# A two-layer attention encoder on one core: block A's value products in two passes of 128 stationary columns, the merging chain a slot later, the first chunk's gate six slots later

## The chip, the cores and the metric

The kernel runs on one core of a Trainium2 chip. PE is the matrix engine (TensorE), DVE the vector engine, ACT the scalar engine, POOL is GpSimd, SP issues the DMAs. The metric is the time of one execution on the device in microseconds (us); of several runs the median counts. 1463.04 us is the median of three runs of the kernel before.

## What is computed

Two encoder layers over x of 1024 positions by 1024 features, all in float32. Each layer normalises x, projects it into the inputs of three attention blocks, A (4 heads), B (6) and C (6), lets each attend, multiplies each block's output by a silu gate and adds the output projection to x. Block A, which the change touches, merges three dilated windows by their log-sum-exp:

```python
DILATED_PATTERNS = ((128, 1), (512, 4), (2048, 16))
for window, dil in DILATED_PATTERNS:
    ...
    m = jnp.max(s, axis=-1, keepdims=True)
    p = jnp.exp(s - m)
    den = jnp.sum(p, axis=-1, keepdims=True)
    o = jnp.einsum('bndhij,bnjdhe->bnidhe', (p / den).astype(v.dtype), vw)
    lse = (m + jnp.log(den))[..., 0]
    ...
w = jax.nn.softmax(jnp.stack(lses, axis=0), axis=0)
out = jnp.sum(w[..., None] * jnp.stack(outs, axis=0), axis=0)
...
y = jnp.concatenate([ya, yb, yc], axis=-1)      # each times its silu gate
x = x + y @ w_out[l]
```

## The kernel before

A float32 operand of a matmul is held as two rounded parts, a high and a low one, and a product is made of three passes: high by high, high by low, low by high. For the values of a head the stationary tile `w` has 128 columns, the 64 high ones in `w[:, LO]` and the 64 low ones in `w[:, HI]`.

Block A treats a head as 8 classes of positions (the four-step pattern, "class" below) and as windows of neighbouring positions. Per head `a_s` makes scores on PE (L897 to L903), DVE adds a table and takes the maximum (L910, L913), `a_exp` is on ACT. The two normalisations are merged by the chain `a_x1` to `a_x5`: DVE L929, PE L937 (a permutation), DVE L944 to L951, ACT L956, DVE L962 to L969 (which gives the window scale `sc` and `z`), PE L977 (the permutation back, from `z`), DVE L983 and L986 (the class scale `s2c`). POOL multiplies the weights by the scales, eight window norms L992 from `sc` and eight class norms L996 from `s2c` for a head. Then PE transposes them, L1009 for classes (`a_t`, i 0 to 3) and L1014 to L1020 for windows (i 4 to 7), each block is split by an ACT copy (L782, L1024) and a DVE subtraction (L783, L1026), and `a_v` multiplies by the values: for classes L1038 to L1040, for windows L1051 to L1053, each line one pass with 64 stationary columns into the 64 low partitions of a PSUM accumulator `acc`:

```python
T.matmul(o, w[:, LO], ph[:, s], start=(kb == 0), stop=False)
T.matmul(o, w[:, LO], pl[:, s], start=False, stop=False)
T.matmul(o, w[:, HI], ph[:, s], start=False, stop=(kb == 1))
```

`a_end` brings an accumulator to SBUF: a class half is copied by ACT (L1085) into the 64 partitions of `y` that belong to the head, a window half is added to it by DVE (L1088, through a strided view). Two heads fill one chunk `fc` of `y`; `fin_gate` multiplies it by its gate on POOL (L820 for block A's chunks 0 and 1, strided; L822 else), `fin_split` splits it (ACT L836, POOL L837). Blocks B and C have `soft` (DVE L762 takes the row maximum of PE's L760 products, ACT L769 the exponential), `norm` (DVE L775, POOL L776), transposes L789 and products L801, L802, and end with two ACT copies (L848, L853) and a POOL add (L854). Early parts of the output projection, `f_load` (a weight piece by DMA, split on POOL by L1103 and L1104) and `f_mm` (PE L1116 to L1118), are put between them.

The order is set by a table: `put(slot, f, pri)` puts a call into a numbered slot, and calls are issued slot by slot, in a slot by priority. A scheduler then settles the order on PE, DVE, POOL and SP; ACT keeps the order written. Block A's head h has its class and window transposes in slots `base_a + AT0 + 8*h + i`, its value products `AV` = 2 slots later, its chain at `CHAIN` (slot offset, priority) behind its last scores, and its norms at fixed slots around the transposes. `FA` are the offsets of a chunk's gate and split.

## Time and profile before

| | |
|---|---|
| median of three runs | 1463.04 us (1462.65 to 1463.38) |
| the profiled execution's own time | 1461.05 us |
| its span in the trace | 1459.1 us |
| PE busy | 1443.1 us (99%), 7912 instructions |
| DVE busy | 1094.5 us (75%), 1997 |
| ACT busy | 899.4 us (62%), 1678 |
| POOL busy | 574.3 us (39%), 516 |

Busy shares are means over the whole span. An engine that is 39% busy can still be the one that others wait for in a stretch. The profiled execution is one run, 2.0 us under the median, and the span is 1.95 us less than its time.

### The profile page before, as it was taken

The page shows a single profiled execution, that of the slowest core. Times are in us where ns is not written, and L with a number is a line of the kernel's source. Part 1 is how long each engine was busy: PE and PEld are TensorE (multiplying, and loading weights), DVE is VectorE, ACT ScalarE, POOL GpSimd, SP SyncE. Part 2 cuts the span into 40 slices and gives each one's busy share as a digit, 9 for nine tenths or more (in the row PEclk, how much of TensorE's full clock was granted, in tenths as well). Part 3 has the DMA queues.
Part 4 walks back from the last instruction along what each step waited for, and adds up shares of the span by engine and source line. Part 5 has one row for each costly group of instructions (what it writes and reads, how often), then busy time and mean ns, then how long its engine had stood idle before and what let it go on. Part 6 is the DMA issues. An engine that isn't in the chain of part 4 may idle for free.

```text
span 1459.1 us, 23134 instructions
## 1 busy us (share of the span) xinstructions
PE 1443.1 (99%) x7912; PEld 1227.4 (84%) x7912; DVE 1094.5 (75%) x1997; ACT 899.4 (62%) x1678; POOL 574.3 (39%) x516
## 2 busy tenths in 40 slices
PE   9999999999999999999999999999999999999999
PEld 7998888888888888888889988888888888888887
DVE  7759767488888789994736597574888787899942
ACT  6473234488888769993425723343888886799820
POOL 6204431135455565550322054211454554754500
PEclk9999999999999999999999999999999999999999
DMA  6261136610287821102622611465103688121143
GB/s 223 80 245 59 52 107 207 207 44 30 51 202 204 243 84 51 44 26 75 212 81 90 238 40 47 166 198 156 59 30 76 172 242 235 31 59 30 44 148 121
DMA packets 118134, 171.81 MB, mean 118 GB/s; under 512 B 11520, under 2 KB 73088, under 8 KB 118016
## 3 DMA queue, kind: packets, MB, share of 16 engines
q1 hardware_dynamic: 118016, 170.32, 38.2%
q8 instruction: 63, 1.03, 0.3%
q14 instruction: 55, 0.45, 0.1%
HBM read 109.47 MB, written 60.82 MB: 117 GB/s over the span
## 4 chain that ended last, share of the span: by engine, by line
PE 90%; DVE 4%; ACT 3%; DMA 1%; issue 1%; SPq 0%; POOL 0%; ACTq 0%; DVEq 0%
PE S L760 15%; PE T L789 11%; PE acc L802 6%; PE acc L801 6%; PE T L669 4%; PE T L667 4%; PE T L668 4%; PE S L1262 3%; PE S L1260 3%; PE S L1261 3%; PE S L221 2%; PE S L222 2%; PE S L223 2%; PE T L705 1%; PE T L221 1%
## 5 line engine op out<-in xcount | busy, mean ns | idle before, releaser
L783 DVE TENSOR_TENSOR wl<-T,wh 128x512 fp32r<-128x512 f32 x440 | 297.0, 685 | 69.2 <-ACT wh L782 67.2
L782 ACT ACTIVATE wh<-T 128x512 fp32r<-128x512 f32 x440 | 261.2, 596 | 115.7 <-PE T L789 77.4
L776 POOL TENSOR_SCALAR u<-u,rec 128x1024 f32<-128x1024 f32 x192 | 216.5, 1128 | 277.4 <-DVE rec L775 176.7
L760 PE MATMUL S<-u,u 96*128 96x512 f32 (+1 forms) x960 | 268.7, 409 | 0.5 <-ACT u L769 0.3
L762 DVE TENSOR_REDUCE nmax<-S 128x1 f32<-128x1024 f32 x192 | 233.7, 1217 | 23.7 <-PE S L760 23.2
L789 PEld LDWEIGHTS T<-ident,u 128*128 128x128 f32 x1536 | 190.8, 140 | 49.0 <-DVE wl L783 0.4
L789 PE MATMUL T<-ident,u 128*128 128x128 f32 x1536 | 230.0, 272 | 0.0
L769 ACT ACTIVATE u<-S,nmax 128x1024 f32<-128x1024 f32 x192 | 213.2, 1111 | 0.3
L150 POOL TENSOR_TENSOR wl<-wr,wh 128x512 fp32r<-128x512 f32 (+2 forms) x48 | 75.1, 1567 | 320.4 <-ACT wh L146 314.9
L760 PEld LDWEIGHTS S<-u,u 96*128 96x128 f32 (+1 forms) x960 | 166.7, 189 | 27.9 <-ACT u L769 1.4
L146 ACT ACTIVATE wh<-wr 128x512 fp32r<-128x512 f32 (+2 forms) x96 | 56.9, 596 | 157.6 <-PE S L222 97.3
L667 PE MATMUL T<-u,wh 128*128 128x512 f32 x256 | 102.1, 399 | 0.0
L669 PE MATMUL T<-u,wl 128*128 128x512 f32 x256 | 100.1, 391 | 0.0
L668 PE MATMUL T<-u,wh 128*128 128x512 f32 x256 | 99.9, 390 | 0.0
L801 PE MATMUL acc<-wh,u 128*128 128x512 f32 x192 | 84.5, 440 | 0.0
L801 PE MATMUL acc<-wh,qb 128*128 128x512 f32 x192 | 82.8, 431 | 0.0
L802 PE MATMUL acc<-wl,u 128*128 128x512 f32 x192 | 76.1, 396 | 2.5 <-DVE wl L783 2.5
L802 PE MATMUL acc<-wl,qb 128*128 128x512 f32 x192 | 76.1, 397 | 0.1
L150 DVE TENSOR_TENSOR wl<-wr,wh 128x512 fp32r<-128x512 f32 (+2 forms) x48 | 41.5, 865 | 44.2 <-ACT wh L146 44.2
L1260 PE MATMUL S<-u,qb 128*128 128x512 f32 x186 | 74.1, 398 | 0.0
L1262 PE MATMUL S<-u,qb 128*128 128x512 f32 x186 | 73.2, 394 | 0.0
L1261 PE MATMUL S<-u,qb 128*128 128x512 f32 x186 | 72.9, 392 | 0.0
(294 smaller groups left out, 3342.0 us busy)
## 6 DMA issues: line engine op xcount, KB each, us to landing
u<-qk_c SPq DMA_DIRECT2D x40, 256.0 KB, 4.1
wr<-in_w_g_dram SPq DMA_DIRECT2D x32, 256.0 KB, 2.6
gates<-h SPq DMA_DIRECT2D x32, 256.0 KB, 2.3
qk_c<-u SPq DMA_DIRECT2D x16, 512.0 KB, 4.0
u<-gates SPq DMA_DIRECT2D x16, 512.0 KB, 3.6
qb<-qk_a SPq DMA_DIRECT2D x32, 256.0 KB, 5.9
vb<-u SPq DMA_DIRECT2D x16, 384.0 KB, 3.3
u<-vb SPq DMA_DIRECT2D x12, 512.0 KB, 4.8
```

The costliest lines, as they stand in the source:

```text
L667: T.matmul(ps[half], wh[:, w], xh[k][:, s], start=(k == 0), stop=False)
L668: T.matmul(ps[half], wh[:, w], xl[k][:, s], start=False, stop=False)
L669: T.matmul(ps[half], wl[:, w], xh[k][:, s], start=False, stop=(k == 7))
L760: T.matmul(ps[:, w], q[:, s], k[:, w], start=(i == 0), stop=(i == len(terms) - 1))
L762: V.tensor_reduce(nmax, ps, op=ALU.max, axis=AX.X, negate=True)
L769: A.activation(p, ps, AF.Exp, bias=nmax, accum_out=den)
L776: G.tensor_scalar(p, p, rec, 1.0, ALU.mult, ALU.mult)
L782: A.activation(ph, ps, AF.Copy)
L783: V.tensor_tensor(pl, ps, f32(ph), ALU.subtract)
L789: T.transpose(ps[:, i * P:(i + 1) * P], Pt[hd, 4 * half + i][0][:, j * P:(j + 1) * P], ident)
L801: T.matmul(acc, w, ph, start=(j == 0), stop=False)
L802: T.matmul(acc, w, pl, start=False, stop=(j == 7))
```

## The change

`a_v` takes the whole of `w` as the stationary tile, so that high and low values are multiplied in one pass, the products of the high values arriving in the accumulator's partitions `LO` and those of the low values in `HI`: two passes instead of three. `a_end` has then to add the two halves of the accumulator. For a class half ACT copies both out and POOL adds them (L1087). For a window half ACT copies `HI` out (strided), DVE adds `LO` to it (L1093) and POOL adds the result to `y` (L1094). The temporary is an `H` tile, of which there are now seven. In `CHAIN` the steps `a_x1p` to `a_x5` go one slot later, `a_x1` stays. For chunk 0 (`h == 1`) `fin_gate` and `fin_split` go six slots later. `f_load` goes three slots later (`FL` 5 instead of 8).

```diff
     def H(dt=F32, shape=(P, 512)):
-        return sp.tile(list(shape), dt, tag="H", name=nm("h"), bufs=6)
+        return sp.tile(list(shape), dt, tag="H", name=nm("h"), bufs=7)
...
-                o = accs["a", h, "c"][LO, (i % 2) * 256:(i % 2) * 256 + 256]
+                o = accs["a", h, "c"][:, (i % 2) * 256:(i % 2) * 256 + 256]
...
-                    T.matmul(o, w[:, LO], ph[:, s], start=(kb == 0), stop=False)
-                    T.matmul(o, w[:, LO], pl[:, s], start=False, stop=False)
-                    T.matmul(o, w[:, HI], ph[:, s], start=False, stop=(kb == 1))
+                    T.matmul(o, w, ph[:, s], start=(kb == 0), stop=False)
+                    T.matmul(o, w, pl[:, s], start=False, stop=(kb == 1))
...
-                T.matmul(o, w[rows, LO], ph[rows, cols], start=start, stop=False, skip_group_check=True)
-                T.matmul(o, w[rows, LO], pl[rows, cols], start=False, stop=False, skip_group_check=True)
-                T.matmul(o, w[rows, HI], ph[rows, cols], start=False, stop=stop, skip_group_check=True)
+                T.matmul(o, w[rows], ph[rows, cols], start=start, stop=False, skip_group_check=True)
+                T.matmul(o, w[rows], pl[rows, cols], start=False, stop=stop, skip_group_check=True)
...
             y = pairs[fc][0]
+            t1 = H()
             if what == "c":
-                A.activation(y[rows, half * 512:half * 512 + 512], acc[LO], AF.Copy)
+                out = y[rows, half * 512:half * 512 + 512]
+                A.activation(t1[rows], acc[HI], AF.Copy)
+                A.activation(out, acc[LO], AF.Copy)
+                G.tensor_tensor(out, out, t1[rows], ALU.add)
             else:
                 yv = y.rearrange("p (r s i) -> p s r i", r=4, s=2)[rows, half]
-                V.tensor_tensor(yv, acc[LO].rearrange("p (i r) -> p r i", r=4), yv, ALU.add)
+                tv = t1[rows].rearrange("p (r i) -> p r i", r=4)
+                lo, hi = (acc[part].rearrange("p (i r) -> p r i", r=4) for part in (LO, HI))
+                A.activation(tv, hi, AF.Copy)
+                V.tensor_tensor(tv, lo, tv, ALU.add)
+                G.tensor_tensor(yv, yv, tv, ALU.add)
...
-        FA = (10, 14)
...
-        CHAIN = ((2, 6), (4, 4.5), (5, 0), (5, 1.5), (6, 0), (8, 4.5), (9, 0))
+        CHAIN = ((2, 6), (5, 4.5), (6, 0), (6, 1.5), (7, 0), (9, 4.5), (10, 0))
...
+                FA = (16, 20) if h == 1 else (10, 14)
...
-        F0, FN, FP, FL = -10, 5, 6.5, 8
+        F0, FN, FP, FL = -10, 5, 6.5, 5
```

POOL, layer 0, from the last class norms of head 1 (L996 from `s2c_5197` before, `s2c_5221` after) to the first of head 2; L992 are head 2's window norms. Before:

```order
L996 TENSOR_SCALAR u_4901<-u_4901,s2c_5197 128x256 x2
L992 TENSOR_SCALAR u_4938<-u_4938,sc_5400 128x192
L992 TENSOR_SCALAR u_4938<-u_4938,sc_5400 128x256
L992 TENSOR_SCALAR u_4999<-u_4999,sc_5400 128x256 x2
L992 TENSOR_SCALAR u_5073<-u_5073,sc_5400 128x256 x2
L992 TENSOR_SCALAR u_5151<-u_5151,sc_5400 128x256
L992 TENSOR_SCALAR u_5151<-u_5151,sc_5400 128x192
L996 TENSOR_SCALAR u_4938<-u_4938,s2c_5502 128x256 x2
```

The same place after; L1094 are the window adds of head 0, L1087 the first class add of head 1:

```order
L996 TENSOR_SCALAR u_4893<-u_4893,s2c_5221 128x256 x2
L1094 TENSOR_TENSOR u_5130<-u_5130,h_5352 64x4x128
L1094 TENSOR_TENSOR u_5130<-u_5130,h_5356 64x4x128
L992 TENSOR_SCALAR u_4934<-u_4934,sc_5416 128x192
L992 TENSOR_SCALAR u_4934<-u_4934,sc_5416 128x256
L992 TENSOR_SCALAR u_4991<-u_4991,sc_5416 128x256 x2
L992 TENSOR_SCALAR u_5056<-u_5056,sc_5416 128x256 x2
L992 TENSOR_SCALAR u_5150<-u_5150,sc_5416 128x256
L992 TENSOR_SCALAR u_5150<-u_5150,sc_5416 128x192
L1087 TENSOR_TENSOR u_5130<-u_5130,h_5433 64x512
L996 TENSOR_SCALAR u_4934<-u_4934,s2c_5523 128x256 x2
```

Nothing stood between the norms of the two heads before; now two adds stand ahead of head 2's window norms and one ahead of its class norms.

POOL, layer 0, from the last class norms of head 2 (L996) to the class norms of head 3; L992 are head 3's window norms, L820 the gates of chunk 0. Before:

```order
L996 TENSOR_SCALAR u_5151<-u_5151,s2c_5502 128x256 x2
L820 TENSOR_TENSOR u_5132<-u_5134,u_5132 128x512 x2
L992 TENSOR_SCALAR u_5221<-u_5221,sc_5645 128x192
L992 TENSOR_SCALAR u_5221<-u_5221,sc_5645 128x256
L992 TENSOR_SCALAR u_5293<-u_5293,sc_5645 128x256 x2
L992 TENSOR_SCALAR u_5382<-u_5382,sc_5645 128x256 x2
L992 TENSOR_SCALAR u_5459<-u_5459,sc_5645 128x256
L992 TENSOR_SCALAR u_5459<-u_5459,sc_5645 128x192
L996 TENSOR_SCALAR u_5221<-u_5221,s2c_5719 128x256 x2
L996 TENSOR_SCALAR u_5293<-u_5293,s2c_5719 128x256 x2
```

The same place after; L1087 and L1094 are the new adds, into `u_5130` for heads 0 and 1 and into `u_5669` for head 2:

```order
L996 TENSOR_SCALAR u_5150<-u_5150,s2c_5523 128x256 x2
L1087 TENSOR_TENSOR u_5130<-u_5130,h_5505 64x512
L1094 TENSOR_TENSOR u_5130<-u_5130,h_5609 64x4x128
L820 TENSOR_TENSOR u_5128<-u_5130,u_5128 128x512
L1094 TENSOR_TENSOR u_5130<-u_5130,h_5613 64x4x128
L820 TENSOR_TENSOR u_5128<-u_5130,u_5128 128x512
L1087 TENSOR_TENSOR u_5669<-u_5669,h_5670 64x512
L992 TENSOR_SCALAR u_5207<-u_5207,sc_5650 128x192
L992 TENSOR_SCALAR u_5207<-u_5207,sc_5650 128x256
L992 TENSOR_SCALAR u_5286<-u_5286,sc_5650 128x256 x2
L992 TENSOR_SCALAR u_5367<-u_5367,sc_5650 128x256 x2
L992 TENSOR_SCALAR u_5452<-u_5452,sc_5650 128x256
```

Where the two gates stood alone ahead of head 3's window norms, they now stand among four adds there, and a fifth, head 2's second class add, comes one row further down, ahead of the last window norm.

DVE, layer 0, from the window sums of head 3's chain (L950) to its scale `sc` (L966) and `z` (L969); L1088 are the last adds of head 1. Before:

```order
L950 TENSOR_TENSOR mm_5613<-st_5219 128x8
L951 TENSOR_TENSOR e_5614<-mm_5613,st_5219 128x16
L783 TENSOR_TENSOR wl_5623<-T_5617,wh_5622 128x512
L1088 TENSOR_TENSOR u_5134<-acc_5543,u_5134 64x4x128
L1088 TENSOR_TENSOR u_5134<-acc_5569,u_5134 64x4x128
L962 TENSOR_TENSOR t_5640<-st_5219,e_5614 128x16
L963 TENSOR_TENSOR rc_5641<-t_5640 128x8
L783 TENSOR_TENSOR wl_5655<-T_5649,wh_5654 128x512
L964 RECIPROCAL rc_5641<-rc_5641 128x8
L966 TENSOR_TENSOR sc_5645<-e_5614,rc_5641 128x16
L969 TENSOR_TENSOR z_5647<-sc_5645,order_2206 128x32
```

The same place after; L1093 are the adds out of PSUM that took the place of L1088, of which the first (it stands one row higher) is left out, L944 and L947 begin head 3's chain step, L762 is a row maximum of block C:

```order
L1093 TENSOR_TENSOR h_5613<-acc_5559,h_5613 64x512
L944 TENSOR_TENSOR z_5619<-T_5601,order_2206 128x32 x2
L783 TENSOR_TENSOR wl_5633<-T_5627,wh_5632 128x512
L947 TENSOR_REDUCE st_5205<-z_5619 128x2x8
L950 TENSOR_TENSOR mm_5623<-st_5205 128x8
L951 TENSOR_TENSOR e_5624<-mm_5623,st_5205 128x16
L962 TENSOR_TENSOR t_5645<-st_5205,e_5624 128x16
L963 TENSOR_TENSOR rc_5646<-t_5645 128x8
L762 TENSOR_REDUCE nmax_5690<-S_5685 128x1
L964 RECIPROCAL rc_5646<-rc_5646 128x8
L783 TENSOR_TENSOR wl_5660<-T_5654,wh_5659 128x512
L966 TENSOR_TENSOR sc_5650<-e_5624,rc_5646 128x16
```

The adds out of PSUM now stand ahead of the chain's step, the four tiny operations L950, L951, L962 and L963 follow each other directly, and a row maximum has come between L963 and L964.

## Rows read from the trace of the kernel before

**Rows 1.** The page's chain of work that ended last, by engine:

```profile
PE 90%; DVE 4%; ACT 3%; DMA 1%; issue 1%; SPq 0%; POOL 0%; ACTq 0%; DVEq 0%
```

**Rows 2.** Stretches: from:to and length in us, then each engine's busy us (instructions), PE clock:

```profile
470.22:489.52 19.30, 19.27 (x138) 17.16 (x136) 16.44 (x62) 13.42 (x47) 15.28 (x26) 1.00 0.96 294
489.52:508.61 19.09, 18.49 (x136) 16.44 (x134) 13.52 (x45) 12.93 (x42) 7.25 (x16) 1.00 0.75 209
508.61:523.25 14.64, 12.41 (x102) 10.96 (x100) 12.82 (x26) 7.40 (x16) 8.58 (x15) 1.00 0.69 196
523.25:536.70 13.45, 13.45 (x105) 12.01 (x104) 11.34 (x19) 10.90 (x21) 8.68 (x10) 1.00 0.01 2
...
1212.82:1231.89 19.07, 18.47 (x135) 16.43 (x134) 13.52 (x45) 12.91 (x42) 7.25 (x16) 1.00 0.71 197
```

**Rows 3.** Timeline of PE: start, us, what; in brackets idle time before and its releaser:

```profile
490.75 0.41 PE L937 MATMUL T<-z,order 128*128 128x64 f32 x2 [0.60 <-DVE wl L1026]
...
509.73 0.41 PE L937 MATMUL T<-z,order 128*128 128x64 f32 x2 [0.50 <-DVE wl L1026]
...
517.95 0.38 PE L977 MATMUL T<-z,order 128*128 128x32 f32 x2 [1.73 <-DVE z L969]
```

**Rows 4.** Timeline of POOL and DVE, 470 to 518 us:

```profile
513.50 3.07 POOL L820 TENSOR_TENSOR u<-u,u 128x512 f32<-128x512 f32 x2 [5.45 <-issue]
...
513.99 1.11 DVE L962 TENSOR_TENSOR t<-st,e 128x16 f32<-128x16 f32 x1
515.13 1.46 DVE L963 TENSOR_TENSOR rc<-t 128x8 f32<-128x8 f32 x1
...
517.40 0.18 DVE L966 TENSOR_TENSOR sc<-e,rc 128x16 f32<-128x16 f32 x1
...
472.01 1.30 POOL L854 TENSOR_TENSOR u<-h,h 64x512 f32<-64x512 f32 x1
...
472.43 0.90 DVE L950 TENSOR_TENSOR mm<-st 128x8 f32<-128x8 f32 x1
```

**Rows 5.** Timeline of PE, passes of 256 columns, and one change of column count:

```profile
475.00 0.28 PE L1040 MATMUL acc<-wh,qb 128*64 128x256 f32 x1
475.12 0.28 PE L1038 MATMUL acc<-wh,qb 128*64 128x256 f32 x1
...
469.38 0.28 PE L898 MATMUL S<-qb,u 128*128 128x256 f32 x1
469.50 0.28 PE L902 MATMUL S<-qb,u 128*128 128x256 f32 x1
...
480.96 0.28 PE L898 MATMUL S<-qb,u 128*128 128x192 f32 x1
481.24 0.30 PE L1038 MATMUL acc<-wh,qb 128*64 128x256 f32 x1
```

**Rows 6.** Groups by line: line, engine, operation, form, count | busy us, mean ns of one:

```profile
L1085 ACT ACTIVATE u<-acc 64x512 f32<-64x512 f32 x16 | 9.4, 590 | 0.6
...
L1088 DVE TENSOR_TENSOR u<-acc,u 64x512 f32<-64x512 f32 x16 | 10.2, 676 | 0.1
...
L762 DVE TENSOR_REDUCE nmax<-S 128x1 f32<-128x1024 f32 x192 | 233.7, 1217 | 23.7 <-PE S L760 23.2
...
L776 POOL TENSOR_SCALAR u<-u,rec 128x1024 f32<-128x1024 f32 x192 | 216.5, 1128 | 277.4 <-DVE rec L775 176.7 <-PE T L789 47.6 <-PE acc L802 21.7
...
L854 POOL TENSOR_TENSOR u<-h,h 64x512 f32<-64x512 f32 x24 | 30.9, 1287 | 14.2 <-ACT h L853 14.1
```

**Rows 7.** Timeline of POOL, norms of head 3:

```profile
517.74 3.57 POOL L992 TENSOR_SCALAR u<-u,sc 128x192 f32<-128x192 f32 x8 [1.17 <-issue]
521.28 3.68 POOL L996 TENSOR_SCALAR u<-u,s2c 128x256 f32<-128x256 f32 x8
```

**Rows 8.** Timeline of PE, head 1's last value matmul, and block C's second half:

```profile
512.21 0.22 PE L1053 MATMUL acc<-wh,qb 64*64 64x128 f32 x1
...
548.75 0.60 PE L789 MATMUL T<-ident,u 128*128 128x128 f32 x4
```

More of the change, by code (lines that the diff above doesn't have):

```diff
@@ L1049, in mm @@
             def mm(half, q0, w, rows, cols, start=False, stop=False):
-                o = accs["a", h, half][LO, q0 * P:q0 * P + (cols.stop - cols.start)]
-                T.matmul(o, w[rows, LO], ph[rows, cols], start=start, stop=False, skip_group_check=True)
-                T.matmul(o, w[rows, LO], pl[rows, cols], start=False, stop=False, skip_group_check=True)
-                T.matmul(o, w[rows, HI], ph[rows, cols], start=False, stop=stop, skip_group_check=True)
+                o = accs["a", h, half][:, q0 * P:q0 * P + (cols.stop - cols.start)]
+                T.matmul(o, w[rows], ph[rows, cols], start=start, stop=False, skip_group_check=True)
+                T.matmul(o, w[rows], pl[rows, cols], start=False, stop=stop, skip_group_check=True)
             full = slice(0, P)
```

## Prediction

> **What bounds the kernel now.** I read the chain of waits first: nine tenths of the chain that ended last lie on PE [rows 1]. So a shorter PE program shortens the kernel wherever nothing else sets the time, and the question is where PE would then wait. Second comes the busy time of each engine by stretch, for the four stretches in which block A's values run [rows 2]. My marks are the first class transposes (L1009) of heads 0 to 3, at 470.22, 489.52, 508.61 and 523.25 us in layer 0, and the first transposes of block C at 536.70. I call the stretches h0 to h3 after the head whose mark begins them; the other layer's h1 repeats within 0.02 us. PE is full in h0 and h3, loses 0.6 us in h1 and 2.2 us in h2. POOL has room in h1 (7.25 of 19.09 us) and less in h2 (8.58 of 14.64) and h3 (8.68 of 13.45). Third, the waits of PE [rows 3]: in h1 and h2 twice 0.5 to 0.6 us at L937, once 1.73 us at L977 until DVE has made z. Fourth, what DVE and POOL did before that 1.73 [rows 4].
>
> **PE: passes removed.** A pass of 256 columns takes 0.12 us from start to start with 64 stationary columns (475.00 to 475.12), and 0.12 with 128 (469.38 to 469.50) [rows 5]. So the two passes left cost what two cost before, and the third is saved whole: 112 passes of 256 columns by 0.117 us and 32 of 128 columns by half of it make 13.1 + 1.9 = 15.0 us for both layers, if nothing takes their place. Going from a 256-column matmul with 128 stationary columns to one with 64 costs 0.28 us instead of 0.12 [rows 5]; I find four such places in a layer, two in h0 and two in h1, 0.16 us each, and they vanish. The 64-row matmuls stay, and what the switch to them costs.
>
> By the order of the two kernels, each stretch has on PE: h0 11 passes of 256 and 2 of 128 columns fewer, but 5 score matmuls (L897 to L903) more, by 0.12: -1.4 + 0.6 = -0.8 us; h1 14 and 4 fewer, and 5 score matmuls fewer: -1.9 - 0.6 = -2.5; h2 14 and 4 fewer, one 512-column matmul more, about -1.65; h3 13 and 4 fewer and one 512-column matmul fewer, about -2.0.
>
> **ACT, DVE, POOL: what a head now ends with.** A block that ended with one ACT copy (0.59 us) or one DVE add out of PSUM (0.68) [rows 6] ends with two ACT copies and a POOL add, or with an ACT copy, the same DVE add and a POOL add. POOL gets 16 adds in a layer. Their nearest row is L854, the same 64x512 add of two SBUF tiles: 1.29 us [rows 6]. The strided gate L820 took 1.54 (two in 3.07) [rows 4] and is the other end. I take 1.29, since the new adds run over rows of 128 or 512 neighbouring elements, as L854 does. 16 by 1.29 are 20.6 us a layer, and what matters is where they stand: L1094 of head 0 and the first L1087 of head 1 ahead of head 2's class norms; the second L1087 and the L1094 of head 1 with both gates L820 and head 2's first L1087 ahead of head 3's window norms.
>
> **h0.** POOL has time before head 1's norms. -0.8 on PE and two column switches, -0.3: **-1.1 us**.
>
> **h1.** -2.5, two column switches -0.3, and the 0.60 us at L937 [rows 3] goes, since the merging is a slot later and L937 no longer follows the class transposes at once: -3.4. Against it POOL: after head 0's last value matmul come the ACT copy and DVE add (1.1 us), two adds (2.6), head 2's eight window norms (3.57 [rows 7]), one add (1.3) and two class norms (0.95, a quarter of 3.68 [rows 7]): 9.5 us until the mark of head 2, where PE has 8.5 us of work and some 0.3 of switching. So PE waits about 0.7 us there (bounds 0 and 1.0): **-2.7 us**.
>
> **h2.** Times are from the start of head 1's last value matmul, 512.21 before; the next mark came 11.0 us later [rows 8]. After: the mark of head 2 lies 2.5 us ahead of it (3.6 before), and POOL is then still in head 2's class norms, six of them after the mark: 2.8 us, to +0.3. Then in a row: L1087 to 1.6, L1094 to 2.9, L820 to 4.4, L1094 to 5.7, L820 to 7.3, L1087 to 8.6. Meanwhile DVE must make head 3's scales: L950, L951, L962, L963, then a row maximum (L762, 1.22 us [rows 6]), L964, a split, L966. Each of the first four is a tiny op of two SBUF inputs. In the trace L962 took 1.11 and L963 1.46 us next to the two L820, each ending within 0.03 us of a POOL op's end, and L950 took 0.90 next to an L854 [rows 4]; such an op alone takes under 0.2 (L966, 0.18 [rows 4]). So with POOL busy without a gap each costs one POOL op. I let L950 go ahead and the other three wait, to 4.4, 5.7 and 7.3; the maximum, a split (about the 0.68 of the add out of PSUM) and the short ops then bring sc at +9.6. POOL does seven window norms (3.1) to 12.7, head 2's second L1087 to 14.0, the last norm to 14.4, two class norms to 15.4: the mark of head 3. The stretch has 2.5 + 15.4 = 17.9 us instead of 14.64: **+3.2 us** (bounds: +2.2 if no op waits, because POOL reaches the window norms only at 8.6; +4.5 if all four wait). The 0.50 and 1.73 us of waits of before are inside the 14.64 and replaced by longer ones at L977 and at the mark.
>
> The Trainium skill, page "SBUF — State Buffer", section "Who interferes with whom", states that a VectorE instruction with two SBUF inputs contends with a GpSimd instruction that reads SBUF, and that the second one blocks fully until the first has ended. By that rule the trace's 1.11, 1.46 and 0.90 us are expected, and it speaks against putting adds on GpSimd here; without it h2 would be at its lower bound, and the total 2.0 us less.
>
> **h3 and the start of block C.** PE has 2.0 us less, but POOL now sets the time to the second half of block C's transposes, which came at 548.75, 25.5 us after the mark of head 3 [rows 8]. POOL has after that mark, up to the eighth softmax norm: six class norms 2.8, eight norms by 1.13 (9.0), six adds (7.7), two splits taken like L854 (2.6), two gates (3.1) [rows 4, 6]: 25.2 us, and I allow 0.1 from the norm's end to the transpose. **-0.2 us**. Behind that block C gives POOL little else than its norms, and nothing is late any more.
>
> **At no cost.** The f_load three slots later stays five slots (some 12 us by h0's 19.3 for eight) ahead of its matmuls. The seventh H buffer serves the new copies. The gates of chunk 0 stand six slots later in the table, but in POOL's order still ahead of head 3's window norms: their 3.1 us are in the sum, and had they come behind, h2 would be 3.1 better and h3 no worse.
>
> **The sum.** -1.1 - 2.7 + 3.2 - 0.2 = -0.8 us a layer, -1.6 in both. The profiled run took 1461.05 (span 1459.1, 1.95 around it), 2.0 under the median of 1463.04; the same step on the median gives **1461.4 us**, with h1's and h2's bounds 1459.0 to 1464.0.
>
> **Rivals.**
> *POOL keeps up.* The tiny DVE ops slip between POOL's, head 2's class norms are there in time, and so POOL starts its row at 1.2 instead of 1.6: h1 -3.4, h2 +1.8, sum -2.9 a layer: 1457.2. For it: POOL is idle for more than half of h1 [rows 2], so head 2's norms have room; against: the three blocked ops of [rows 4], and that POOL's six ops stand back to back.
> *All that PE saves arrives:* 15.0, the three waits of [rows 3] (2.83 a layer, 5.7), the column switches (1.3): -22.0, 1441.0. For it: PE bounds the chain; against: POOL has 42 us of its own work from the mark of head 2 to block C's second half, where 40.1 us passed before.
> *The adds are longer, slower than before.* An add of 1.57 us, as the gate L820 about took, is 0.28 more, and 14 of them a layer stand in the POOL rows counted above (3 in h1, 5 in h2, 6 in h3): +3.9, sum +3.1 a layer, 1469.2. It turns from gain to loss at an add of 1.35 us, and is slower by 0.2% from 1.45. For it: they write into half the partitions of a strided view; against: L854 does so too.
>
> **How the numbers follow.** A measurement tells about 0.2% (2.9 us) from no change: faster is under 1460.1, slower over 1466.0. Forecast 0.50 (of it 0.10 under 1460.1), POOL keeps up 0.26, all arrives 0.08, longer adds 0.16. Faster: 0.10 + 0.26 + 0.08, less 0.02 for the slow end of the first rival, is 0.42; slower 0.15 (the longer adds but 0.01); same 0.43. The range leaves out all arrives and half of the longer adds, and takes the others: 1455.0 to 1467.5.
>
> **What would show it.** L1038 to L1040's third pass gone and 0.12 us a pass of 128 columns: the PE term. A wait at the first L1009 of head 2 that ends with POOL: h1. L951, L962, L963 over 1 us each and a wait of some 4 us at L977 or the matmul ahead of it: the price in h2; short ones there make the first rival. L1087 and L1094 near 1.29 us or near 1.57: the last. Stretches of 18.2, 16.4, 17.9 us between the marks: each term. Wrong altogether I would be if the marks did not depend on POOL: if the norms ran before the adds or PE found other work at L977.

## The result and the profile after

The changed kernel takes 1473.8 us (median of 4 runs, 1472.61 to 1475.41) where the kernel before took 1462.85 beside it: a ratio of 1.0083, interval 1.0070 to 1.0096. It is slower by 10.9 us. The forecast was 1461.4 and its range ended at 1467.5.

First the stretches of the changed kernel between the same marks as in [rows 2] (from:to and length, then busy us and instructions of PE, PEld, DVE, ACT and POOL, then PE's granted clock). They are h0, h1, h2, h3 and, last, from block C's first transposes to its second half:

```profile
470.10:491.24 21.14, 19.06 (x130) 16.42 (x128) 15.13 (x63) 14.85 (x49) 16.68 (x26) 1.00 1.03 296
491.24:510.31 19.07, 17.56 (x111) 14.84 (x111) 13.47 (x44) 15.24 (x46) 13.13 (x25) 1.00 0.77 211
510.31:526.67 16.36, 13.77 (x82) 11.57 (x82) 13.63 (x28) 9.43 (x18) 13.74 (x18) 0.90 0.64 187
526.67:540.75 14.08, 13.07 (x85) 11.02 (x85) 10.53 (x16) 12.70 (x22) 13.74 (x16) 1.00 0.05 15
540.75:552.73 11.98, 11.98 (x70) 9.84 (x71) 10.96 (x19) 10.65 (x22) 10.36 (x9) 1.00 0.07 28
```

Together they are 82.63 us; before they were 78.53 (from 470.22 to 548.75, [rows 2, 8]). The four heads should have shrunk by what PE no longer does; h0 grew by 1.8 us, h1 stayed, h2 grew by 1.7 and h3 by 0.6. The other layer repeats this to 0.02 us. So 8.2 of the 11.7 us by which the span grew lie between the marks; 0.9 per layer follow directly behind (a PE wait of 0.76 us at 553.97, below), and some 1.7 us come between there and the second layer's marks, about 1.0 of them by the first scores of that layer. Those 1.7 were not traced further.

PE's longest waits in these stretches and directly behind them (start, us, what; in brackets the idle time before and its releaser), to be held against [rows 3]:

```profile
478.86 0.51 PE L1123 MATMUL T<-u,h 128*128 128x512 f32 x1 [0.72 <-POOL u L837]
481.79 0.36 PE L1038 MATMUL acc<-wh,qb 128*128 128x256 f32 x1 [0.83 <-ACT wh L782]
486.20 0.30 PE L1014 MATMUL T<-ident,u 128*128 128x128 f32 x1 [0.43 <-DVE wl L783]
510.31 0.63 PE L1009 MATMUL T<-ident,u 128*128 128x128 f32 x4 [1.05 <-DVE wl L783]
518.01 0.39 PE L1038 MATMUL acc<-wh,qb 128*128 128x256 f32 x1 [0.76 <-ACT wh L782]
520.45 0.39 PE L1039 MATMUL acc<-wl,qb 128*128 128x256 f32 x1 [0.54 <-DVE wl L783]
522.04 0.43 PE L977 MATMUL T<-z,order 128*128 128x32 f32 x2 [0.97 <-DVE z L969]
539.93 0.38 PE L1050 MATMUL acc<-wh,qb 128*128 128x256 f32 x1 [0.35 <-ACT wh L782]
540.75 0.63 PE L789 MATMUL T<-ident,u 128*128 128x128 f32 x4 [0.43 <-DVE wl L783]
553.97 0.33 PE L789 MATMUL T<-ident,u 128*128 128x128 f32 x1 [0.76 <-POOL u L776]
```

The two waits at L937 are gone, as forecast. The one at L977, forecast to grow to some 4 us, shrank from 1.73 to 0.97. Beside it stand new ones of 0.35 to 1.05 us, and most end with ACT or DVE: with the split of a transposed block (L782 and L783), which I had not thought to be late. h0, where PE was full, now has three.

The page's chain [rows 1] doesn't help here: after the change it breaks off, and its shares sum to 14% only.

**POOL and DVE in h2**, which carried most of the forecast (timelines; [rows 4] is the same place before):

```profile
510.63 1.28 POOL L1087 TENSOR_TENSOR u<-u,h 64x512 f32<-64x512 f32 x1
514.07 1.29 POOL L1094 TENSOR_TENSOR u<-u,h 64x512 f32<-64x512 f32 x1 [2.16 <-DVE h L1093]
515.44 1.55 POOL L820 TENSOR_TENSOR u<-u,u 128x512 f32<-128x512 f32 x1
517.07 1.29 POOL L1094 TENSOR_TENSOR u<-u,h 64x512 f32<-64x512 f32 x1
518.44 1.56 POOL L820 TENSOR_TENSOR u<-u,u 128x512 f32<-128x512 f32 x1
519.96 1.27 POOL L1087 TENSOR_TENSOR u<-u,h 64x512 f32<-64x512 f32 x1
```

```profile
515.82 1.20 DVE L950 TENSOR_TENSOR mm<-st 128x8 f32<-128x8 f32 x1
...
517.50 0.89 DVE L962 TENSOR_TENSOR t<-st,e 128x16 f32<-128x16 f32 x1 [0.28 <-ACT e L956]
518.42 0.17 DVE L963 TENSOR_TENSOR rc<-t 128x8 f32<-128x8 f32 x1
...
520.31 0.96 DVE L966 TENSOR_TENSOR sc<-e,rc 128x16 f32<-128x16 f32 x1
521.79 0.20 DVE L969 TENSOR_TENSOR z<-sc,order 128x32 f32<-128x32 f32 x1
```

The adds and gates stand in the order forecast, with a gap of 2.16 us after the first, and three tiny operations take 0.9 to 1.2 us each, though they are L950, L962 and L966, not L951, L962 and L963. The adds have the length taken: 16 at L1087 with a mean of 1.278 us and 16 at L1094 with 1.291 ([rows 6] has L854).

So the mechanism that was worked out in most detail came about, and yet h2 has only 1.7 of the 4.1 us a layer. The experiments look for the rest. All were timed in several rounds beside the kernel before. A gain or loss in us is the difference of the medians, the kernel before taking 1461.7 to 1462.9 us beside each; ratios and intervals come from runs paired by round and can differ from it by 0.1%.

### The profile page after: what moved, and what is told of

Same layout as the page of the kernel before. It is cut to its first block, busy times and chain, and to the rows that moved or that the text cites. A ratio compares the mean times of both kernels' runs of the same rounds, so it can differ in the third digit from the quotient of the medians.

```text
span 1470.8 us, 22941 instructions
## 1 busy us (share of the span) xinstructions
PE 1443.6 (98%) x7768; PEld 1222.1 (83%) x7768; DVE 1091.4 (74%) x1997; ACT 918.9 (62%) x1710; POOL 613.7 (42%) x548
## 5 line engine op out<-in xcount | busy, mean ns | idle before, releaser
L783 DVE TENSOR_TENSOR wl<-T,wh 128x512 fp32r<-128x512 f32 x440 | 297.1, 686 | 82.7 <-ACT wh L782 81.2
L776 POOL TENSOR_SCALAR u<-u,rec 128x1024 f32<-128x1024 f32 x192 | 215.9, 1125 | 264.7 <-DVE rec L775 155.3
L782 ACT ACTIVATE wh<-T 128x512 fp32r<-128x512 f32 x440 | 260.9, 596 | 99.6 <-PE T L789 77.5
L762 DVE TENSOR_REDUCE nmax<-S 128x1 f32<-128x1024 f32 x192 | 233.7, 1217 | 24.2 <-PE S L760 23.7
```

Of the source, the lines that this page charges most:

```text
L762: V.tensor_reduce(nmax, ps, op=ALU.max, axis=AX.X, negate=True)
L776: G.tensor_scalar(p, p, rec, 1.0, ALU.mult, ALU.mult)
L782: A.activation(ph, ps, AF.Copy)
L783: V.tensor_tensor(pl, ps, f32(ph), ALU.subtract)
```

## The experiments

**1. Which part costs.** e1 has the two passes and the new ending of a block with the old table, e2 the new table alone, e3 the two passes alone (the old ending, which takes only the lower half `LO` of the accumulator, so the products of the low values are computed but left out), and e12 the passes and the table with that old ending.

```diff
# e1: the changed kernel with
-        CHAIN = ((2, 6), (5, 4.5), (6, 0), (6, 1.5), (7, 0), (9, 4.5), (10, 0))
+        CHAIN = ((2, 6), (4, 4.5), (5, 0), (5, 1.5), (6, 0), (8, 4.5), (9, 0))
-                FA = (16, 20) if h == 1 else (10, 14)
+                FA = (10, 14)
-        F0, FN, FP, FL = -10, 5, 6.5, 5
+        F0, FN, FP, FL = -10, 5, 6.5, 8
# e2: the kernel before with these three the other way round
# e12: the changed kernel with the old a_end; e3: e1 with the old a_end
-                A.activation(t1[rows], acc[HI], AF.Copy)
...
-                V.tensor_tensor(tv, lo, tv, ALU.add)
-                G.tensor_tensor(yv, yv, tv, ALU.add)
+                V.tensor_tensor(yv, acc[LO].rearrange("p (i r) -> p r i", r=4), yv, ALU.add)
```

> The two passes and the new ending of a block, with the table of before (chain, gate and f_load where they were; seven H buffers). Theory 1, the adds on POOL and what waits for POOL cost the time: about as slow as the changed kernel, 1470 to 1477, with L962 and L963 over 1 us beside POOL adds. Theory 2, the table of slots costs it (the ACT queue stands behind a later L956, matmuls of the early output projection stand ahead of their split): under 1463, some 1455. Theory 3, the longer ending of a block (two more steps on ACT and DVE before the accumulator's bank is free) costs it, wherever the adds are: 1468 to 1475.

> Three passes and the ending of before, with the changed table alone (chain a slot later, gate of chunk 0 six slots later, f_load three slots later). Theories 1 and 3: within 3 us of before, 1460 to 1466. Theory 2: slower by 5 to 12 us, 1468 to 1475.

> Two passes, but the block ends as before, with the high half alone: the products with the low part of the values are left out of the result. The table is that of before. It measures what the passes alone are worth. If all that PE saves arrives: 1441 to 1448. If waits of other engines take it (the chain of merging, POOL's norms): 1452 to 1460. No theory expects over 1463.

> The two passes with the changed table and the ending of before (the low half of the values left out). With the same passes and ending the table of before took 1455.8; the table alone costs 3.9 us. If the costs add: 1457 to 1461, and then ACT's copies (1464.9 with them) and POOL's adds (1464.5 with them) cost 4 to 8 us each and both together 13 to 17. If either of the two alone already costs nearly all and the kernels with one of them are held by something else: 1463 to 1466.

| kernel | us | against before, interval | h0 | h1 | h2 | h3 | to C's second half |
|---|---|---|---|---|---|---|---|
| before | | | 19.30 | 19.09 | 14.64 | 13.47 | 12.03 |
| e3, passes | 1455.75 | 0.9956, 0.9941 to 0.9971 | 18.66 | 17.88 | 15.24 | 12.05 | 11.80 |
| e2, table | 1466.18 | 1.0028, 1.0017 to 1.0039 | 21.57 | 18.76 | 14.17 | 13.79 | 12.04 |
| e12, passes and table | 1458.17 | 0.9975, 0.9964 to 0.9986 | 20.65 | 18.52 | 12.50 | 12.76 | 11.79 |
| e1, passes and ending | 1483.22 | 1.0146, 1.0131 to 1.0161 | 22.07 | 20.54 | 18.93 | 14.48 | 11.31 |
| after, all three | 1473.8 | 1.0083, 1.0070 to 1.0096 | 21.14 | 19.07 | 16.36 | 14.08 | 11.98 |

The passes alone gain 6.6 us, the table alone loses 3.9, both together gain 3.5. The new ending then costs 14.4 us (from -3.5 to +10.9). With the old table it costs even 27.5 (from -6.6 to +20.9): the table is there for the ending, it gives 10 us back with it and loses 3 to 4 without it. In e1 PE waits 4.57 us for `z` at 524.82, and behind that its granted clock is 0.50, the level of 1.2 GHz:

```profile
525.00:530.00 5.00, 5.00 (x24) 5.00 (x25) 1.83 (x5) 2.35 (x5) 5.00 (x13) 0.50 0.02 8
```

**2. What of the ending costs.** e10 leaves the POOL adds out (the copies of the low half stay, and nothing adds them), e11 leaves the new ACT copies out (POOL adds a tile to itself), e4 adds both halves on DVE out of PSUM, without POOL and without the copies of `HI`. e13 is e10 with two fills of 64x512 on POOL, 0.52 us each, in place of each add: they write but read nothing. e14 is the changed kernel with the pass of the low weights done twice, so PE has three passes again.

```diff
# e10
-                G.tensor_tensor(out, out, t1[rows], ALU.add)
...
-                V.tensor_tensor(tv, lo, tv, ALU.add)
-                G.tensor_tensor(yv, yv, tv, ALU.add)
+                V.tensor_tensor(yv, lo, yv, ALU.add)
# e11
-                A.activation(t1[rows], acc[HI], AF.Copy)
-                G.tensor_tensor(out, out, t1[rows], ALU.add)
+                G.tensor_tensor(out, out, out, ALU.add)
# e4
+                V.tensor_tensor(out, acc[HI], out, ALU.add)
...
+                for part in (LO, HI):
+                    V.tensor_tensor(yv, acc[part].rearrange("p (i r) -> p r i", r=4), yv, ALU.add)
# e13: e10, and behind each block
+                    for _ in range(2):
+                        G.memset(t1[rows], 0.0)
# e14
+                    T.matmul(o, w, pl[:, s], start=False, stop=False)
```

> The changed kernel with the same copies on ACT and the same adds on DVE, but without the adds on POOL: the low half of the values is copied and then left out of the result. Theory 1, the adds on POOL cost the time: 1460 to 1466. Theory 3, the longer ending on ACT and DVE costs it: 1470 to 1475. Theory 4, split copies on ACT queue behind an exponential L956 that waits for DVE, which waits for POOL: 1464 to 1469, with the idle time of ACT ahead of L956 shorter than the 2.42 us of the changed kernel.

> The changed kernel with the POOL adds (each adds the tile to itself, so the result is not the sum of the halves), but with the copies and adds of before on ACT and DVE: no ACT copy of the low half. Theory 1: 1470 to 1476, as slow as the changed kernel. Theory 3: 1458 to 1464. Theory 4: 1466 to 1472, since ACT still waits at L956 for DVE and POOL, but with fewer copies behind it.

> The changed kernel with the halves added by DVE out of PSUM instead of by POOL: a class half is one ACT copy and one DVE add, a window half two DVE adds; no new POOL instruction, no ACT copy more than before, 32 DVE adds of about 0.68 us more. Theory 1: 8 to 14 us faster than the changed kernel, 1460 to 1466. Theory 2: within 3 us of the changed kernel, 1471 to 1477. Theory 3: 2 to 6 us faster, 1468 to 1472, since ACT has fewer copies and DVE more.

> The kernel without POOL adds (1464.9), with two fills of a 64x512 tile on POOL in the place of each add: POOL is occupied there but reads no SBUF (the low half is left out of the result). If the adds cost by occupying POOL's queue: 1471 to 1476 where the two fills last about as long as an add (1.29 us), in proportion where they are shorter, and L950, L962, L966 blocked as before. If they cost by blocking DVE's operations of two SBUF inputs: 1463 to 1467, with L950 and L962 of head 3 under 0.2 us.

> The changed kernel with the second pass of every product made twice (the low part of the weights counted twice in the result): PE has as many passes as before, with the new ending and the changed table. If PE's waits of the changed kernel would have hidden the third pass, since other engines set the time: 1473 to 1477, no slower than the two passes. If the passes' 15 us are worth the 6.6 us that they brought with the old ending: 1478 to 1482. If all of them count: 1486 to 1490.

| kernel | us | ratio, interval | gain or loss | h0 | h1 | h2 | h3 |
|---|---|---|---|---|---|---|---|
| e12, old ending | 1458.17 | 0.9975, 0.9964 to 0.9986 | -3.5 | 20.65 | 18.52 | 12.50 | 12.76 |
| e10, ACT copies | 1464.92 | 1.0025, 1.0014 to 1.0037 | +2.8 | 21.13 | 19.01 | 13.73 | 14.07 |
| e11, POOL adds | 1464.47 | 1.0017, 1.0008 to 1.0026 | +2.4 | 20.66 | 18.51 | 14.46 | 12.87 |
| e13, copies and fills | 1470.97 | 1.0067, 1.0050 to 1.0084 | +9.3 | 21.15 | 19.11 | 15.30 | 14.12 |
| e4, DVE adds | 1474.00 | 1.0081, 1.0064 to 1.0098 | +11.7 | 20.44 | 19.56 | 16.14 | 14.15 |
| e14, three passes | 1478.18 | 1.0111, 1.0096 to 1.0126 | +16.5 | 22.35 | 19.12 | 15.66 | 16.39 |

The 32 further ACT copies alone cost 6.3 us, the 32 POOL adds alone 5.9, both 14.4. So the copies, to which the forecast gave no term of their own, cost as much as the adds, on which it spent most of its working. The 2.2 us that are left, which would come only from both together, are within the noise of these differences. By stretch (h0 to h3) the copies cost 0.5, 0.5, 1.2 and 1.3 us (e12 to e10); the 0.5 in h0 is no wait but four score matmuls more that PE does there. The adds on top of them (e10 to the changed kernel) cost 2.6 us in h2 and under 0.1 in each other stretch, then 1.0 directly behind, where the wait of 0.76 at 553.97 is. DVE in the place of both does no better (+11.7). e14 says what the third pass is worth with this ending: leaving it out gains 5.6 us (16.5 to 10.9).

e13 asks what it is about the adds. From e10 to the changed kernel 1.29 us of adding a time cost 8.1 us; 1.04 us of filling, 0.81 of that time, cost 6.5. That is 0.80 of the cost by the medians, 0.72 by the paired ratios and 0.62 by the spans of the two profiled executions (4.9 of 7.9 us). So more than half of the cost comes with POOL being taken, though the fills read nothing. What the reading and the blocking of DVE cost beside that isn't separated. The gates L820 still read in e13, and beside one of them (517.57 to 519.11) L963 takes 1.50 us where it took 0.17 after the change (DVE of e13):

```profile
517.63 1.50 DVE L963 TENSOR_TENSOR rc<-t 128x8 f32<-128x8 f32 x1
```

And in h2, where the fills cost 1.6 us and the adds 2.6, PE's granted clock is 1.00 with the fills and 0.90 with the adds, so a part of the difference can be the clock.

**3. Is it the order?** e6 takes only the chain of the changed kernel back, e9 keeps that chain and moves its exponential one slot further, with the step behind it, e19 moves the class copies a slot later, behind the exponentials. e17 and e18 are the kernels before and after with POOL's order as the table writes it, without the scheduler. e20 queues head 1's window adds and head 2's class adds behind the last class norm of head 3, and the gates behind the eighth norm of block C.

```diff
# e6
-        CHAIN = ((2, 6), (5, 4.5), (6, 0), (6, 1.5), (7, 0), (9, 4.5), (10, 0))
+        CHAIN = ((2, 6), (4, 4.5), (5, 0), (5, 1.5), (6, 0), (8, 4.5), (9, 0))
# e9
+        CHAIN = ((2, 6), (5, 4.5), (6, 0), (7, 1.5), (7, 1.7), (9, 4.5), (10, 0))
# e19
-                    a_end(h, "c", i // 2)
+                    put(base_a + AT0 + 8 * h + i + AV + 1, lambda: a_end(h, "c", i // 2), 9)
# e17, e18
-    ctx.enter_context(tc.manual_schedule(engines={mybir.EngineType.Activation}))
+    ctx.enter_context(tc.manual_schedule(engines={mybir.EngineType.Activation, mybir.EngineType.Pool}))
# e20 (behind: issued after the named norm)
+            if (h, what) in ((1, 0), (1, 1), (2, "c")):
+                put(base_a + 30, lambda: behind(("c", 3), f), 9)
...
+                FA = (33, 37) if h == 1 else (14, 18)
```

> The changed kernel with the merging chain where it stood before, the other moves kept. The two passes with the new ending took 1483.2 with the table of before and 1473.8 with the new one. If the chain's slot brings that difference: 1480 to 1484. If the gate of chunk 0 or f_load brings it: 1472 to 1476. With the table of before the one wait that grew most was at L977 for z (6.9 us): that wait comes back if the chain's slot is the cause.

> The changed kernel with the exponential L956 of the merging chain written behind the next split copy in ACT's order instead of ahead of it (and the step after it as much later in the same slot). Nothing is added or removed. Theory 4: 3 to 6 us faster than the changed kernel, 1468 to 1471, and the waits of PE for ACT's split at L1038 (0.83 and 0.76 us in layer 0) gone. Theories 1 and 3: within 2 us of it or slower, 1472 to 1478, since the merging chain ends later.

> The changed kernel with the two ACT copies of a class half one slot later, behind the next exponentials L920 and L922 in ACT's order (and the adds behind them). If the copies cost by standing ahead of the exponentials and the splits: 3 to 6 us faster than the changed kernel, 1467.5 to 1471, and the wait of 1.05 us at the first L1009 of head 2 gone. If they cost by holding the accumulator's bank longer: slower than it, 1475 to 1480.

> The kernel before with POOL's instructions in the order written in the table (as ACT's are), not in the scheduler's: class norms of a head come ahead of its window norms, the gates of chunk 0 behind head 3's first norms. The same instructions on every engine. If the norms' place in POOL's queue sets part of the time of before: 1455 to 1460. If not: 1461 to 1466.

> The changed kernel with POOL's instructions in the order of the table: class norms ahead of window norms, the new adds and the gates of chunk 0 mostly behind them. If the adds cost by standing in the queue ahead of norms that PE waits for: 5 to 10 us faster than the changed kernel, 1463 to 1468. If they cost by occupying POOL and blocking DVE wherever they stand: 1471 to 1476.

> The changed kernel with some POOL instructions queued later: the window adds of head 1 and the class adds of head 2 behind head 3's last class norm, both chunks' gates behind the eighth norm of block C. Nothing is added or removed. If the adds cost by their place ahead of the norms: 4 to 8 us faster than the changed kernel, 1466 to 1470, its stretch from the mark of head 2 to that of head 3 at 13.7 us (as without any POOL add) instead of 16.36, and no tiny DVE operation of head 3 over 0.5 us. If POOL's occupation sets the time wherever the adds stand: 1472 to 1475, what is won there lost again ahead of block C.

| kernel | us | ratio, interval | gain or loss |
|---|---|---|---|
| e6, chain back | 1478.02 | 1.0118, 1.0103 to 1.0133 | +15.9 |
| e9, exponential later | 1475.57 | 1.0102, 1.0087 to 1.0118 | +13.5 |
| e19, copies later | 1479.94 | 1.0116, 1.0100 to 1.0133 | +18.0 |
| e17, before, POOL as written | 1472.12 | 1.0070, 1.0053 to 1.0087 | +10.2 |
| e18, after, POOL as written | 1491.41 | 1.0197, 1.0182 to 1.0212 | +29.5 |
| e20, adds and gates behind norms | 1474.09 | 1.0085, 1.0066 to 1.0104 | +12.4 |

No order tried for this ending is better than the one it has. e6 shows what the later chain is for. Its timeline of DVE, POOL and PE (h2 is 20.70 us there):

```profile
521.99 3.37 DVE L969 TENSOR_TENSOR z<-sc,order 128x32 f32<-128x32 f32 x1
...
521.39 1.26 POOL L1087 TENSOR_TENSOR u<-u,h 64x512 f32<-64x512 f32 x1
522.64 3.54 POOL L992 TENSOR_SCALAR u<-u,sc 128x192 f32<-128x192 f32 x8
...
525.51 0.61 PE L977 MATMUL T<-z,order 128*128 128x32 f32 x2 [6.84 <-DVE z L969]
```

An operation of 128x32 elements, 0.20 us elsewhere, takes 3.37: it begins beside an add and ends only after most of the eight norms that follow without a gap, and PE stands 6.84 us. By this the tiny operation can lose to several POOL operations in a row. The Trainium skill, page "SBUF — State Buffer", section "Who interferes with whom", says that a VectorE instruction with two SBUF inputs contends with a GpSimd instruction that reads SBUF, and not with one that only writes. The traces agree with the first half: 3.37 us here, 0.89 for L962 in the changed kernel, 1.50 for L963 beside a gate in e13. For the second half they have little: L962 in e13 began 0.07 us before the end of a fill and took 0.18.

e20 puts the theory to the test that the adds cost time because of their place ahead of the norms. Its stretches h2 and to C's second half, and the longest wait of PE in the last:

```profile
510.99:523.71 12.72, 12.19 (x82) 10.11 (x82) 10.45 (x27) 9.25 (x18) 5.63 (x12) 1.00 0.82 241
...
536.83:553.63 16.80, 13.78 (x71) 11.08 (x72) 11.27 (x19) 10.67 (x22) 12.79 (x12) 0.90 0.00 1
```

```profile
540.58 0.33 PE L796 MATMUL T<-ident,u 128*128 128x128 f32 x1 [2.23 <-POOL u L776]
```

h2 is 3.6 us shorter than after the change (12.72 for 16.36) and h3 1.0 (13.12 for 14.08), and all of it is given back: 16.80 for 11.98, because the adds now stand between block C's norms (L776), and PE waits for these. With 16 more adds a layer POOL's time was short wherever they were put. That theory fell; POOL's occupation, to which e13 points, stands.

**4. The two passes with a cheaper ending.** e15 keeps the two passes and ends a block with one ACT copy (class) or one DVE add (window) over all 128 partitions, as many instructions as before. The half that lies in the wrong partitions is moved by a DMA from SBUF to SBUF, and POOL adds once for both heads of a chunk, 128x512, ahead of each gate: 4 adds a layer for 16. The chain and `FL` are those of before, the gates and their splits come later (`FA` 20 and 24 for chunk 0, 12 and 16 for chunk 1). e16 is e15 with POOL's order as written and the gates later. e21 is e15 with the gates of chunk 1 and the splits of chunk 0 later still, and with chunk 0's sums and gates issued behind the last class norm of head 3, chunk 1's behind the eighth norm of block C.

```diff
# e15
+            if what == "c":
+                A.activation(y[:, half * 512:half * 512 + 512], acc, AF.Copy)
+                return
+            yv = y.rearrange("p (r s i) -> p s r i", r=4, s=2)[:, half]
+            V.tensor_tensor(yv, acc.rearrange("p (i r) -> p r i", r=4), yv, ALU.add)
...
+                nc.sync.dma_start(z[LO], yv[HI])
...
+                nc.sync.dma_start(z[HI], yv[LO])
+                nc.sync.dma_start(e[HI], yv[HI])
...
+            G.tensor_tensor(yv, yv, Zs.pop((fc, half)).rearrange("p (r i) -> p r i", r=4), ALU.add)
# e21: e15, and
+                    put(..., lambda h=h, half=half: behind(("c", 3) if h == 1 else (("c", 0), 7), lambda: fin_gate(h // 2, half)), 6)
```

> A version that may beat both: two passes, the table of before but for chunk 0's gate, and a block that ends on all 128 partitions at once: one ACT copy or one DVE add as before, both halves kept, the other head's half exchanged by DMA, and one POOL add of 128x512 ahead of each gate, 4 a layer instead of 16. If ACT's copies and POOL's adds set the cost: 1455 to 1460. If the fewer passes are worth nothing as soon as any adds stand on POOL ahead of head 3's window norms, or if the DMAs come late: 1463 to 1470.

> The version with the halves exchanged by DMA (1466.6; there POOL's add and gate of chunk 0 stand ahead of head 3's class norms, and PE waits 1.93 us at L1010 and 2.97 at L789 for POOL), with POOL in the order of the table and the gates later. If POOL's queue ahead of the norms is the cause of these waits: 1453 to 1459, faster than both kernels. If occupation is: 1463 to 1468.

> The version with the halves exchanged by DMA and four POOL adds a layer (1466.6), with chunk 0's adds and gates queued behind head 3's last class norm and chunk 1's behind block C's eighth norm; otherwise the scheduler's order. The waits for POOL there were 1.93 and 2.97 us in layer 0. If they go: 1456 to 1460, faster than both kernels by more than 0.2% of the one before at the lower half. If block C's norms wait for POOL elsewhere: 1462 to 1466.

| kernel | us | ratio, interval | gain or loss | h0 | h1 | h2 | h3 | to C's second half |
|---|---|---|---|---|---|---|---|---|
| e15 | 1466.61 | 1.0039, 1.0025 to 1.0052 | +4.9 | 18.24 | 17.68 | 14.97 | 15.28 | 11.35 |
| e16 | 1471.48 | 1.0065, 1.0049 to 1.0080 | +9.6 | 22.01 | 17.34 | 12.94 | 14.36 | 11.34 |
| e21 | **1451.67** | 0.9928, 0.9913 to 0.9942 | **-10.1** | 18.26 | 17.65 | 13.05 | 13.35 | 11.35 |

e15's h0 and h1 are 1.1 and 1.4 us shorter than before, a little more than the passes alone brought (e3, 0.6 and 1.2); ACT and DVE get no more instructions than before. But with its gates and sums ahead of the norms it loses that in h2, h3 and behind (PE waits 1.93 us for a class norm at 521.10 and 2.97 for a norm of block C at 551.19). e21 has the same sums and gates behind the norms, and there place decides, since POOL has time to give. Its last three stretches, as above:

```profile
506.03:519.08 13.05, 11.56 (x80) 9.92 (x81) 10.44 (x25) 6.01 (x12) 5.05 (x13) 1.00 0.96 263
519.08:532.43 13.35, 12.97 (x86) 11.19 (x87) 11.32 (x21) 10.70 (x23) 12.19 (x13) 1.00 0.50 144
532.43:543.78 11.35, 11.34 (x68) 9.50 (x69) 10.26 (x18) 9.29 (x18) 5.84 (x6) 1.00 0.49 113
```

PE is full in h0 (18.17 of 18.26 us), h1 (17.59 of 17.65) and the last, and POOL is busy for 23.1 us of these three stretches where the changed kernel has 37.8. It beats both kernels by 10 and 22 us. One thing isn't shown by it: whether the gates behind the norms would also help the kernel before, which has no such run. That part of the 10 us may be theirs is open.

## Why the prediction was wrong

The steps that failed are prices. The table was put "at no cost" and costs 3.9 us alone (e2). ACT's 32 further copies had no term of their own and cost 6.3 (e12 to e10). PE's saving, put at 15.0 us, is some 11.5 by the spacings below. The term worked out with most care, POOL in h2, was the right mechanism with too large a size.

In the profile the forecast was -0.8 us a layer between the marks and nothing behind; it was +4.1, +0.9 directly behind, and some 0.8 more a layer in the untraced rest. By stretch, forecast and measured: h0 -1.1 and +1.8; h1 -2.7 and 0.0; h2 +3.2 and +1.7; h3 with block C's start -0.2 and +0.6.

**PE: passes removed.** The counts held, and the 256-column pass too (0.12 us). The 128-column term was mis-sized. Here are three such passes before, with 64 stationary columns, and three after, with 128 (timelines of PE, to be read from start to start):

```profile
489.15 0.22 PE L1051 MATMUL acc<-wh,qb 128*64 128x128 f32 x1
489.21 0.22 PE L1052 MATMUL acc<-wl,qb 128*64 128x128 f32 x1
489.28 0.22 PE L1053 MATMUL acc<-wh,qb 128*64 128x128 f32 x1
```

```profile
508.71 0.22 PE L1050 MATMUL acc<-wh,qb 128*128 128x128 f32 x1
508.77 0.27 PE L1051 MATMUL acc<-wl,qb 128*128 128x128 f32 x1
508.88 0.27 PE L1050 MATMUL acc<-wh,qb 128*128 128x128 f32 x1
```

0.06 us became 0.11 (but for the first, which follows a pass of 256 columns), so three passes at 0.06 and two at 0.11 cost about the same; the 64-row ones go from 0.32 us for three to 0.37 or 0.42 for two. The 32 passes I took to save 1.9 us cost 1 to 2 us more instead (16 of 64 rows by 0.05 to 0.10, 16 of 128 rows by 0.02 to 0.04), and by this estimate PE's saving is 11 to 12 us, not 15.0. I had priced 128 columns at "half of it" without a row. The Trainium skill, page "TensorE: Matmul & The Clock Gate", section "LDWEIGHTS (loading the stationary operand)", gives the load of the stationary tile a time in ns of its columns divided by 1.2, by which I estimate 53 ns for 64 and 107 for 128. The spacing of 0.06 and 0.11 agrees with that; the weight loads themselves are longer in the profile (129 to 135 ns for 64 columns, 183 to 210 for 128). The passes of 256 columns, at 0.12 us with either, don't show it.

**"At no cost"** is the step that failed first. The table was held to move work without touching PE; the chain's slot had only a gain in the sum, the wait at L937. e2, the table alone, makes h0 longer by 2.3 us, with PE waiting at the same three places as after the change (0.29 us for POOL L837, 1.04 for ACT L782, 0.65 for DVE L783). The first two hang on ACT, which keeps the order written. First its L836 waits 3.68 us for POOL's gate L822, and POOL's L837 waits for L836; before, ACT had no wait there. L822 stands behind head 0's norms, which with the later chain begin 4.7 us ahead of the mark of h0 in e2 and 6.0 ahead of it before. Then the chain's tiny exponential (L956) waits for DVE, and the split of a block that PE needs is queued behind it (timeline of ACT after):

```profile
476.82 0.63 ACT L836 ACTIVATE u<-u 128x512 fp32r<-128x512 f32 x1 [3.68 <-POOL u L822]
...
480.02 0.22 ACT L956 ACTIVATE e<-e 128x16 f32<-128x16 f32 x1 [1.10 <-DVE e L951]
...
481.13 0.57 ACT L782 ACTIVATE wh<-T 128x512 fp32r<-128x512 f32 x1
```

PE's L1038 at 481.79 waits for that split. I had asked who waits for the chain, and not what is queued behind its waiting instruction. But that is not the whole cause: in e9, where L956 stands behind this split, PE waits at neither L1038 nor L1123, and h0 is 21.20 us all the same, with waits of 0.46, 0.39 and 0.41 us for DVE in their place. Which of the table's three moves costs the 2.3 us wasn't separated either: with the chain alone back (e6) h0 is 20.72 us for 21.14, so the chain's slot is at most a part. So the cause within the table stays open. The sum of h0 closes: the passes give 0.9 with this table (e2 to e12) and the copies cost 0.5 (e12 to e10), 2.3 - 0.9 + 0.5 = 1.9 for the 1.8 measured.

**h1.** PE's own sum fell as forecast (17.2 to 14.8 us by the shortest spacings of its matmuls), the wait at L937 went, and yet the stretch has the old length: the gaps rose from 1.9 to 4.3 us. The forecast wait at the mark of head 2 is there, 1.05 us, but its releaser is not POOL's norm. It is a split, and behind it again ACT (ACT and DVE after):

```profile
507.31 0.59 ACT L1086 ACTIVATE u<-acc 64x512 f32<-64x512 f32 x1
...
508.87 0.57 ACT L782 ACTIVATE wh<-T 128x512 fp32r<-128x512 f32 x1
...
509.48 0.69 DVE L783 TENSOR_TENSOR wl<-T,wh 128x512 fp32r<-128x512 f32 x1 [0.22 <-ACT wh L782]
```

The two class copies (L1085 from 506.70 and L1086) stand ahead of two exponentials on ACT, its split L782 behind these, and DVE's split L783 waits last for L782. e10, which has the copies without the adds, has the same wait (1.04 us, from DVE); e11, without the copies, has none there and an h1 0.5 us shorter. With the copies a slot later (e19) the wait at the mark goes too, but h1 is 20.04 us, with waits at other places. So no better place for them was found: the new copies are 32 times 0.59 us of ACT, 19 us, that the two passes don't give back there. The other gaps are small ones, all but one under 0.3 us, in some twenty places, and passes alone gained 1.2 us of the 2.7 here (e3). I had counted the copies once, as the lead time of POOL's row, and not as load on ACT.

**h2.** The mechanism was right and its size too large: the mark of head 3 came 13.6 us after head 1's last value matmul, not 15.4, since `sc` was there at +8.2 and not +9.6. And without POOL's adds the stretch would have come to 13.73 us and without the copies either to 12.50, below the 14.64 of before: the place had more to gain than I credited. What the sum didn't have is the clock. Behind the waits of 0.76 and 0.54 us and around that of 0.97 PE was granted in part its 2.4 GHz and in part its 1.2 (stretch, as above; clock 0.69):

```profile
521.00:526.50 5.50, 4.38 (x22) 3.91 (x21) 4.48 (x11) 3.48 (x7) 5.37 (x11) 0.69 0.03 9
```

5.5 us at 0.69 are up to 1.7 us lost against the full clock. In e10, e11 and e12 it is 1.00 from 508 to 530 us.

**h3 and block C.** 26.06 us passed for 25.2 of counted POOL work, and that near agreement is luck: up to the mark of block C's second half it is not POOL that PE waits for. Its waits at 539.93 and 540.75 end with splits, and ACT's split stands behind two class copies and a split of chunk 0 (ACT after):

```profile
538.14 0.59 ACT L1086 ACTIVATE u<-acc 64x512 f32<-64x512 f32 x1
538.76 0.63 ACT L836 ACTIVATE u<-u 128x512 fp32r<-128x512 f32 x1
539.29 0.58 ACT L782 ACTIVATE wh<-T 128x512 fp32r<-128x512 f32 x1
```

Without any POOL add the two stretches take the same 26.03 us (e10, 14.07 and 11.96); with the adds and without the copies they take 24.68 (e11, 12.87 and 11.81). POOL's eighth norm, due 25.2 us after the mark of head 3, ended after 27.2, with 2 us of idle POOL in between. "Nothing is late any more" behind the mark was wrong: PE waits for that norm (L776) at 553.97.

**The rivals.** None of them came. *The adds are longer* ended on the right side by the wrong route: they take 1.28 and 1.29 us. *POOL keeps up* fell with the blocked operations. *All that PE saves arrives* is false of this ending; e21 comes to -10.1 us, of which the share of the later gates is open. Missing was the rival that the ACT copies cost as much as the adds, with 6.3 us as its price (e12 to e10), and the range had no room for it.

## What to carry to other kernels

Before a pass is taken off the bounding engine, price what its result costs to collect, in instructions on every other engine that feeds it: 32 copies of 0.6 us cost as much here as 32 adds of 1.3. Ask of each instruction that waits on an in-order engine what stands behind it, the tiny ones too. No order tried here hid 32 adds; a few can be hidden, once they stand behind the work that others wait for (15 us between e15 and e21).

## What the runs showed of the hardware

- A DVE operation of 0.20 us with two SBUF inputs can take 3.37 us while POOL runs operations without a gap (L969 in e6).
- A pass of 128 moving columns is spaced by its stationary columns, 0.06 us for 64 and 0.11 for 128; one of 256 is not.
- The granted clock was lower around a row of waits each under 1 us (0.69 in 5.5 us), as it was behind one wait of 4.57 (0.50).
- DMAs between partitions of SBUF replaced the copies: e21 moves 173.5 MB for the 170.3 of before and is 10.1 us faster.
